# A hybrid mLSTM / DeltaNet decoder block: output travels on another DMA queue, and new due times for the steps of the triangular inverse

## The chip, the cores and the metric

The kernel runs on one core of a Trainium2 chip. TensorE (PE) multiplies matrices and loads its stationary operand (PEld); VectorE (DVE), ScalarE (ACT) and GpSimd (POOL) do the elementwise work; SyncE (SP) issues DMAs. [...] The metric is the device time of one execution in microseconds. The kernel before takes 2387.58 us (median of 3 runs, 2386.59 to 2389.55).

## The reference

One decoder layer over 512 tokens of width 2048, all in float32. The input is normalised and projected by one matrix `w_in`; the columns feed two token mixers and two merge gates.

```python
u = _rmsnorm(h, norm_w)
proj = jnp.matmul(u, w_in)
...
h_a = _mlstm_chunkwise(...)          # 8 heads, key width 128, value width 256
h_a = _merge_heads(_rmsnorm(h_a)) * ml_norm_w
h_a = h_a * jax.nn.sigmoid(ml_o) * jax.nn.silu(ml_z)

qkv = _causal_conv_silu(dn_qkv, dn_conv_w)   # width-4 causal convolution, then silu
dq, dk_ = _l2norm(dq), _l2norm(dk_)          # 16 heads of width 128
h_b = _gated_delta_chunkwise(dq, dk_, dv_, beta, g)
h_b = _merge_heads(_rmsnorm(h_b, dn_norm_w)) * jax.nn.silu(dn_z)

y_a = jnp.matmul(h_a, w_out[:ML_WIDTH])
y_b = jnp.matmul(h_b, w_out[ML_WIDTH:])
return sigmoid(gate_a) * y_a + sigmoid(gate_b) * y_b
```

The result is added to the input and normalised once more. The delta rule in a chunk needs the inverse of a unit lower triangular matrix, `I + A` with `A` made of the products of keys:

```python
a_mat = jnp.where(strict, bc[..., :, None] * kk * decay_mat, 0.0)
sol = lax.linalg.triangular_solve(a_mat + eye, rhs, lower=True, unit_diagonal=True)
```

## The kernel before

**Weights.** Every weight matrix is streamed once. A tile of 256 KB (`wr`) is loaded by SP, split into a high part `wh` by ACT (`split_hi`) and a rest `wl` by DVE (`split_lo`), and each product is made three times, high x high, high x low, low x high (L222 to L224, L252 to L254, L972 to L974). There are 768 such tiles, four buffers of `wr` and four of each part. The loop that emits the program loads four tiles and splits three tiles ahead of the one that PE is on.

**Units.** Work goes in units: four mLSTM units (two heads each) and eight DeltaNet units (two heads each), in the order m, d, d, m, d, d, and so on; so a DeltaNet unit is the first or the second of its pair. A unit projects its columns in blocks of eight weight tiles (`proj_cm`; in a DeltaNet unit K, Q, V, Z), where the two PSUM tiles of a block are taken from three buffers: the second head's first product of a block needs the first head's PSUM tile of the block before, which ACT must have copied out (`yp`, L451; `gz` and `thz`, L469 and L471). After the units come the merge gates (four narrow blocks, `proj_tm`, then six wide ones) and the output projection.

**Ticks.** The rest of a unit (norms, decay matrices, the inverse, the recurrences, output norm) is written as generators. `start(gen, wait)` files one, `tick()` is called after each half of a weight tile (six wide matmuls), and a generator's `yield n` asks to be resumed n ticks later. So the source says at which tick each small step is emitted. PE runs in exactly the order in which its instructions are emitted. For the other engines and for the DMA queues a planner reorders by its own estimates and by priority: `urgent()` raises it, `behind("A")` and `behind("V")` say that an instruction may not stand ahead of the newest split on ACT or DVE. Each queue then runs strictly in the planned order.

**A DeltaNet unit.** With tick 0 at the end of block K:
- `conv_silu` and `silu_end` (filed 3 and 5 ticks after their block for the two heads) make k, then `turn` makes a token-major copy. A turn is a transpose of 32 x 32 blocks on DVE, and then a trip through DRAM (`travel`): four stores `td` and, four ticks later, one load back. All of these DMAs are in SP's queue.
- `dn_front_k` makes the decay matrices, the products k·k (`pk`), the diagonal blocks `ls` (through DRAM, `ld`), and from tick 16 on the inverse of 128 small triangles, 31 steps of two DVE instructions each (`tmp`, `xi`; L573, L575). The result goes through DRAM (`xd`, L583; `tt`, L584), and 10 ticks later DVE turns it into `tn` (L587).
- `dn_front_q`, filed 8 ticks after block Q, makes the products k·q (`pqk`, L595).
- `dn_back`, filed 4 ticks after block Z, first takes the norms of q on ACT (`token_norms`, 64 squares in all units), then completes the inverse by four rounds of small products on PE (`p1` to `p4`; the first, L629, reads `tn`), with copies by ACT and DVE between them (`s1`, `tb`, `ta`, `s3`).
- `dn_chain` runs the recurrence of a head over its four chunks, normalises, and turns the output `os_` (`to`); `gated` multiplies it by the gate TURN ticks later and SP stores it to `h_d`.

**An mLSTM unit** ends in `ml_fin`, which turns two output tiles of each head (`mhn`) and files `gated` for each.

In all, 32 output tiles (16 `mhn`, 16 `to`) and 56 others (keys, queries, values) travel.

Of the kernel before, what the change touches and what calls it, by code (L numbers as in the profile page):

```python
# [17 lines left out]
NC = S // P  # L18
# [8 lines left out]
GNARROW = 4  # L27
GLAG = 3
KLAST = 4
TURN = 12  # L30
KWAIT, QWAIT = 4, 8
EPS = 1e-6
CAP = 15.0
MLH, DNH = 8, 16
# [5 lines left out]
BS = 32  # L40
# [8 lines left out]
def hybrid_body(  # L49
# [16 lines left out]
    nc = tc.nc  # L66
    ctx.enter_context(tc.manual_schedule(engines={mybir.EngineType.PE}))
    V, A, G, T = nc.vector, nc.scalar, nc.gpsimd, nc.tensor
# [51 lines left out]
    def behind(eng):  # L120

        return tc.issue_after(newest[eng])
# [56 lines left out]
    def urgent(level=1):  # L179
        return tc.high_priority(offset=level * PRIO)  # L180
# [4 lines left out]
    def start(gen, wait=0):  # L185
        active.append([gen, clock["t"] + wait])
# [242 lines left out]
    for i in range(NYP):  # L429
        t = wk.tile([P, S + 3], F32, tag=f"yp{i}", name=f"yp{i}", bufs=1)  # L430
# [13 lines left out]
    def bc(col, n):  # L444
        return col.unsqueeze(2).to_broadcast([P, NC, n])
# [11 lines left out]
    def silu_end(dst, then=None):  # L457
        th = wk.tile([P, S], F32, tag="th", name="th", bufs=3)
        with behind("A"):
            A.activation(th, dst, AF.Tanh)  # L460
        V.scalar_tensor_tensor(out=dst, in0=th, scalar=1.0, in1=dst, op0=ALU.add, op1=ALU.mult)
        if then is not None:
            turn(*then)
        yield 1
# [13 lines left out]
            with urgent():  # L478
                A.activation(jk, pk[:, c, :], AF.Square, accum_out=dst[:, c:c + 1])

    def turn(src, dst):


        o = dst if dst is not src else wk.tile([P, NC, P], F32, tag="to", name="to", bufs=2)
        V.transpose(o if len(src.shape) == 3 else o.rearrange("p n c -> p (n c)"), src)
        start(travel(o, dst), 2)

    def travel(o, dst):
        d = dr.tile([16, BS, 4, BS], F32, tag="td", name="td", bufs=8)
        ov = o.rearrange("p n (j c) -> p (n j) c", c=BS)  # L490
        with urgent(2):
            for a in range(4):
                nc.sync.dma_start(d[:, :, a, :].rearrange("m r c -> r m c"), ov[a * BS:(a + 1) * BS])
        yield 4
        with urgent(2):
            nc.sync.dma_start(dst, d.rearrange("(n j) r a c -> (j r) n (a c)", n=NC))
        yield 1

    def gated(hn, w, g, kt):
# [6 lines left out]
    def dn_front_k(hs, kq, u):  # L506
        rbs = [row_bcast(16 + h, "gb") for h in hs]
        yield 4
        for j in range(2):
# [1 line left out]
            G.affine_select(out=dm, in_=rbs[j], pattern=[[0, NC], [1, P]], channel_multiplier=-1, base=0,  # L511
                            compare_op=ALU.is_ge, fill=-1e30)
            u["dm"].append(dm)
        yield 2
        for j in range(2):
            h, rb, dm = hs[j], rbs[j], u["dm"][j]
            ge = wk.tile([P, NC], F32, tag="ge", name="ge", bufs=4)
# [50 lines left out]
        for i in range(BS - 1):  # L568
            n, m = BS - 1 - i, i // 4 + 1
# [11 lines left out]
        with urgent():  # L581
            for q in range(4):
                nc.sync.dma_start(xd[:, :, :, q, :].rearrange("g b m t -> (g b) m t"), xi[q * NSYS:(q + 1) * NSYS])  # L583
            nc.sync.dma_start(tt, xd.rearrange("g b m q t -> (b m q) g t"))  # L584
        yield 10
        with urgent(), behind("V"):
            V.transpose(tn.rearrange("p g m -> p (g m)"), tt.rearrange("p g t -> p (g t)"))  # L587
        u.update(tn=tn, tt=tt)
# [1 line left out]
    def dn_front_q(hs, kq, u):  # L590
        for j in range(2):
# [8 lines left out]
            G.tensor_tensor(out=qt, in0=qt, in1=eg, op=ALU.mult)  # L600
            u["qt"].append(qt)
            yield 1

    def dn_back(hs, kq, u):

        qe = wk.tile([P, 2, NC], F32, tag="qe", name="qe")
        with behind("A"):
            for j in range(2):
                token_norms(u["qn"][j], qe[:, j, :])
        V.tensor_scalar(out=qe, in0=qe, scalar1=EPS, scalar2=EPS * P, op0=ALU.add, op1=ALU.mult)  # L610
        u["qe"] = qe
        for j in range(2):
            ke = u["ke"][j]
            G.tensor_tensor(out=ke, in0=ke, in1=bc(u["dm"][j][0][:, :, P - 1], P), op=ALU.mult)


        tn, tt = u["tn"], u["tt"]
        G2 = [(j * NC + c, u["aq"][j][:, c, 0, :]) for j in range(2) for c in range(NC)]
        for b in range(4):
            bs = slice(b * BS, (b + 1) * BS)  # L620
            G.tensor_copy(tb[bs, :, bs], tt[bs])
        for b in range(2):
            bs = slice(b * BS, (b + 1) * BS)
            G.tensor_copy(ta[bs, :, bs], tn[bs])
        p1 = psw.tile([P, 2 * NC, BS], F32, tag="wk", name="p1")
        for g, a in G2:
            for q in range(2):
                a0, a1 = slice(64 * q, 64 * q + 32), slice(64 * q + 32, 64 * q + 64)
                T.matmul(p1[a1, g, :], a[a0, a1], tn[a0, g, :], start=True, stop=True)  # L629
        s1 = wk.tile([P, 2 * NC, BS], F32, tag="s3", name="s1", bufs=1)  # L630
        for q in range(2):
            a1 = slice(64 * q + 32, 64 * q + 64)
            with urgent():
                A.mul(s1[a1], p1[a1], -1.0)
        yield 2
        p2 = psw.tile([P, 2, 2 * NC, BS], F32, tag="wk", name="p2")
        for g, a in G2:
            for q in range(2):
                a0, a1 = slice(64 * q, 64 * q + 32), slice(64 * q + 32, 64 * q + 64)
                T.matmul(p2[a0, 0, g, :], s1[a1, g, :], tt[a1, g, :], start=True, stop=True)  # L640
            T.matmul(p2[32:64, 1, g, :], tt[32:64, g, :], s1[32:64, g, :], start=True, stop=True)
        for q in range(2):
            a0, a1 = slice(64 * q, 64 * q + 32), slice(64 * q + 32, 64 * q + 64)
            with urgent():
                A.copy(tb[a0, :, a1], p2[a0, 0])
        with urgent():
            V.tensor_copy(ta[32:64, :, 0:32], p2[32:64, 1])
        yield 2
        p3 = psw.tile([P, 2 * NC, 64], F32, tag="wk", name="p3")
        for g, a in G2:  # L650
            T.matmul(p3[64:128, g, :], a[0:64, 64:128], ta[:, g, :], start=True, stop=True)
        s3 = wk.tile([P, 2 * NC, 64], F32, tag="s3", name="s3", bufs=1)
        with urgent():
            A.mul(s3[64:128], p3[64:128], -1.0)
        yield 2
        p4 = psw.tile([P, 2 * NC, 64], F32, tag="wk", name="p4")
        for g, a in G2:
            T.matmul(p4[0:64, g, :], s3[64:128, g, :], tb[64:128, g, 64:128], start=True, stop=True)
        with urgent():
            V.tensor_copy(tb[0:64, :, 64:128], p4[0:64])  # L660
        for j in range(2):
            vn = u["vs"][j]
            with behind("V"):
                V.tensor_tensor(out=vn, in0=vn, in1=bc(u["nk"][:, j, :], P), op=ALU.mult)
        start(dn_chain(0, hs, kq, u), 2)
        start(dn_chain(1, hs, kq, u), 3)

    def dn_chain(j, hs, kq, u):
        h = hs[j]
        aq, qt, ke, ge = u["aq"][j], u["qt"][j], u["ke"][j], u["dm"][j][2]  # L670
# [5 lines left out]
        for c in range(NC):  # L676
            tsl = slice(c * P, (c + 1) * P)
            if st is None:
                r = vn[:, c, :]
            else:  # L680
                pr = psw.tile([P, P], F32, tag="wk", name="pr")
                T.matmul(pr, kq[j][:, 0, tsl], st, start=True, stop=True)
                r = wk.tile([P, P], F32, tag="r", name="r")
# [34 lines left out]
        os_ = wk.tile([P, NC, P], F32, tag="os", name="os")  # L718
        with urgent():
            V.tensor_tensor(out=os_, in0=po, in1=bc(rsd, P), op=ALU.mult)  # L720
        turn(os_, os_)
        start(gated(os_, normc[:, 32:33], u["g"][j], KT + h), TURN)

    def dn_unit(p):
        hs = (2 * p, 2 * p + 1)
        dcol = p * NB
        u = {"aq": [], "qt": [], "ke": [], "vs": [], "g": [], "dm": []}
        kq = [wk.tile([P, 2, S], F32, tag="kq", name=f"kq{h}", bufs=4) for h in hs]
        ps = proj_cm(DN_K + dcol)
        for j in range(2):  # L730
            ke = wk.tile([P, NC, P], F32, tag="ke", name="ke", bufs=4)
            u["ke"].append(ke)
            conv_silu(ps[j], 16 + hs[j], kq[j][:, 0, :])
            start(silu_end(kq[j][:, 0, :], (kq[j][:, 0, :], ke)), 3 + 2 * j)
        start(dn_front_k(hs, kq, u), 1)
        ps = proj_cm(DN_Q + dcol)
        u["qn"] = []
        for j in range(2):
            conv_silu(ps[j], hs[j], kq[j][:, 1, :])
            qn = wp.tile([P, NC, P], F32, tag="tg", name="qn", bufs=3)  # L740
            u["qn"].append(qn)
            start(silu_end(kq[j][:, 1, :], (kq[j][:, 1, :], qn)), 3 + 2 * j)
        start(dn_front_q(hs, kq, u), QWAIT)
        ps = proj_cm(DN_V + dcol)
        for j in range(2):
            vt = wk.tile([P, NC, P], F32, tag="vn", name="vt", bufs=4)
            u["vs"].append(vt)
            conv_silu(ps[j], 32 + hs[j], vt.rearrange("p c t -> p (c t)"))
            start(silu_end(vt.rearrange("p c t -> p (c t)"), (vt, vt)), 3 + 2 * j)
        ps = proj_cm(DN_Z + dcol)  # L750
        for j in range(2):
            g = wk.tile([P, S], F32, tag="g", name="gz", bufs=4)
            silu2(ps[j], g)
            u["g"].append(g)
        start(dn_back(hs, kq, u), 4)

    def ml_prep(j, hs, kq, u):
        h = hs[j]
# [72 lines left out]
    def ml_fin(j, hs, u):  # L831
        h = hs[j]
        hm = u["hm"][j]
        for i in range(2):
            hn = wk.tile([P, NC, P], F32, tag="os", name="mhn")
            turn(hm[i], hn)
            kt = 2 * h + i
            start(gated(hn, normc[:, 16 + kt:17 + kt], u["g"][j][i], kt), TURN)
            yield 1
# [118 lines left out]
    for nb in range(D // NO):  # L958
        nsl = slice(nb * NO, (nb + 1) * NO)
        for br in range(2):  # L960
# [3 lines left out]
            for c in range(NC):  # L964
                pool, t = (wp, "tg") if br == 0 or c == 3 else (bp, "tgb")
# [73 lines left out]
```

## Time and profile before

| what | us |
|---|---|
| median of 3 runs (lowest, highest) | 2387.58 (2386.59, 2389.55) |
| the profiled execution, its span | 2387.62, 2385.8 |
| PE busy | 2308.0 (97%) |
| DVE, ACT, POOL busy | 1146.0, 802.2, 198.2 |
| DMA: share of the 16 engines, over the span | 47.2%, 130 GB/s |
| mean granted TensorE clock | 0.988 |

The page gives the busy time of each engine; an engine is busy while one of its instructions runs, also when its clock is reduced. The list of waits says which instruction stood idle before it could start, what ended the wait, how long in total, how often, and the longest. A timeline line gives start, length, engine, source line, operation, output and inputs, and in brackets the idle time before it. SPq and ACTq are the DMA issues of those queues: their length is the time of the issue, not of the transfer.

The median time from issue to landing is 2.8 us for a weight tile, 2.7 us for one of the stores `td`, and 3.2 (`mhn`) or 3.6 us (`os`) for the load back of an output.

### The profile page before, as it was taken

Reading aid. Unit: us, or ns where it says so; the run is one execution under the profiler, and the core shown is the slowest. Engines: PE = TensorE matmul, PEld = TensorE weight load, DVE = VectorE, ACT = ScalarE, POOL = GpSimd, SP = SyncE. Lnnn points to the kernel's source line nnn. Section 1 sums busy time; section 2 is a strip of 40 time slices with the busy share of each in tenths; the row PEclk is TensorE's granted clock in tenths of the full one; section 3 lists DMA queues with packets and bytes.
Section 4 is the critical chain, followed back from the end, with each engine's and each line's share of the span. In section 5 each row is a group of like instructions: output and inputs, shape, how many; then the busy total and the mean of one; then the engine's idle time right before and its main releaser. Section 6 shows DMA issues by size and latency. Waiting matters only on the chain. (4 is left out here: it accounts for less than half of the span.)

```text
span 2385.8 us, 32124 instructions
## 1 busy us (share of the span) xinstructions
PE 2308.0 (97%) x11647; PEld 1926.1 (81%) x11647; DVE 1146.0 (48%) x2331; ACT 802.2 (34%) x1702; POOL 198.2 (8%) x277
## 2 busy tenths in 40 slices
PE   6999989999998999999899999989999999999998
PEld 5888877878887777888787888878998888888886
DVE  4532857533385743248583325857333222444334
ACT  4333333333333333233333324434333323322222
POOL 0000202100020200002020001111000000010010
PEclk9999999999999999999999999999999999999999
DMA  4433555443365645336563534646374533633333
GB/s 146 130 97 98 142 139 142 126 128 98 101 153 126 154 112 133 97 98 163 127 167 93 137 97 113 168 105 164 96 246 145 159 115 120 212 115 121 126 115 129
DMA packets 465441, 313.12 MB, mean 131 GB/s; under 512 B 234113, under 2 KB 404322, under 8 KB 465282
## 3 DMA queue, kind: packets, MB, share of 16 engines
q1 hardware_dynamic: 465218, 311.01, 47.2%
q8 instruction: 91, 1.49, 0.2%
q14 instruction: 68, 0.56, 0.1%
q10 hardware_dynamic: 64, 0.07, 0.0%
HBM read 264.77 MB, written 46.20 MB: 130 GB/s over the span
## 5 line engine op out<-in xcount | busy, mean ns | idle before, releaser
L118 DVE TENSOR_TENSOR wl<-wr,wh 128x512 fp32r<-128x512 f32 x768 | 547.3, 714 | 910.9 <-ACT wh L115 887.9
L115 ACT CAST wh<-wr 128x512 fp32r<-128x512 f32 x768 | 476.9, 622 | 1286.7 <-PE pj L223 586.4
L222 PE MATMUL pj<-uh,wh 128*128 128x512 f32 x1792 | 735.9, 411 | 13.3 <-ACT yp L451 7.9
L223 PE MATMUL pj<-ul,wh 128*128 128x512 f32 x1792 | 705.1, 393 | 0.3 <-DVE ul L304 0.3
L224 PE MATMUL pj<-uh,wl 128*128 128x512 f32 x1792 | 705.2, 394 | 0.0
L222 PEld LDWEIGHTS pj<-uh,wh 128*128 128x128 f32 x1792 | 340.5, 190 | 83.2 <-ACT yp L451 10.0
L224 PEld LDWEIGHTS pj<-uh,wl 128*128 128x128 f32 x1792 | 340.0, 190 | 74.1
L223 PEld LDWEIGHTS pj<-ul,wh 128*128 128x128 f32 x1792 | 341.1, 190 | 64.6 <-DVE ul L304 0.8
L972 PE MATMUL py<-wh,hh 128*128 128x512 f32 x512 | 199.2, 389 | 0.0
L973 PE MATMUL py<-wl,hh 128*128 128x512 f32 x512 | 199.2, 389 | 0.0
L974 PE MATMUL py<-wh,hl 128*128 128x512 f32 x512 | 199.2, 389 | 0.0
L253 PE MATMUL pg<-wl,uh 128*128 128x512 f32 x384 | 149.5, 389 | 0.2 <-DVE wl L118 0.2
L252 PE MATMUL pg<-wh,uh 128*128 128x512 f32 x384 | 149.5, 389 | 0.0
L254 PE MATMUL pg<-wh,ul 128*128 128x512 f32 x384 | 149.4, 389 | 0.0
L973 PEld LDWEIGHTS py<-wl,hh 128*128 128x128 f32 x512 | 96.1, 188 | 20.1
L974 PEld LDWEIGHTS py<-wh,hl 128*128 128x128 f32 x512 | 96.1, 188 | 19.9
L972 PEld LDWEIGHTS py<-wh,hh 128*128 128x128 f32 x512 | 96.1, 188 | 19.8
L252 PE MATMUL pv<-wh,uh 128*128 128x512 f32 x256 | 99.6, 389 | 0.0
L253 PE MATMUL pv<-wl,uh 128*128 128x512 f32 x256 | 99.6, 389 | 0.0
L254 PE MATMUL pv<-wh,ul 128*128 128x512 f32 x256 | 99.6, 389 | 0.0
L253 PEld LDWEIGHTS pg<-wl,uh 128*128 128x128 f32 x384 | 72.1, 188 | 15.3 <-DVE wl L118 0.5
L252 PEld LDWEIGHTS pg<-wh,uh 128*128 128x128 f32 x384 | 72.1, 188 | 15.1
(243 smaller groups left out, 2319.2 us busy)
## 6 DMA issues: line engine op xcount, KB each, us to landing
wr<-in_w_in_dram SPq DMA_DIRECT2D x640, 256.0 KB, 2.8
wr<-in_w_out_dram SPq DMA_DIRECT2D x128, 256.0 KB, 2.9
td<-to SPq DMA_DIRECT2D x128, 64.0 KB, 2.7
hr<-h_d SPq DMA_DIRECT2D x32, 256.0 KB, 3.4
tgl<-tg_d SPq DMA_DIRECT2D x32, 256.0 KB, 3.1
tg_d<-tgw SPq DMA_DIRECT2D x24, 256.0 KB, 3.3
xt<-in_x_dram SPq DMA_DIRECT2D x8, 512.0 KB, 8.2
gb<-rows_d SPq DMA_DIRECT2D x16, 256.0 KB, 3.5
```

What stands on the lines that cost most here:

```text
L115: newest["A"] = A.copy(hi, src).ins
L118: newest["V"] = V.tensor_tensor(out=lo, in0=src, in1=hi.bitcast(F32), op=ALU.subtract).ins
L222: T.matmul(ps[j], hi[:, k, wsl], uh[:, kt, :], start=(kt == 0), stop=False)
L223: T.matmul(ps[j], hi[:, k, wsl], ul[:, kt, :], start=False, stop=False)
L224: T.matmul(ps[j], lo[:, k, wsl], uh[:, kt, :], start=False, stop=(kt == KT - 1))
L252: T.matmul(ps[c], uh[:, kt, tsl], hi[:, 0, :], start=(kt == 0), stop=False)
L253: T.matmul(ps[c], uh[:, kt, tsl], lo[:, 0, :], start=False, stop=False)
L254: T.matmul(ps[c], ul[:, kt, tsl], hi[:, 0, :], start=False, stop=(kt == KT - 1))
L972: T.matmul(ps[c], hh[base][:, kt, tsl], hi[:, 0, :], start=(kt == 0), stop=False)
L973: T.matmul(ps[c], hh[base][:, kt, tsl], lo[:, 0, :], start=False, stop=False)
L974: T.matmul(ps[c], hl[base][:, kt, tsl], hi[:, 0, :], start=False, stop=(kt == KT - 1))
```

## The change

- `turn` takes a flag `out`. For the 32 output tiles the five DMAs of a travel are issued by ACT, each set tied behind ACT's newest split, and the travel begins 3 ticks after the transpose and no longer 2. The 56 other travels stay with SP.
- `dn_front_k` waits one tick more before its exponentials (2 to 3) and four more between the inverse's DMAs and `tn` (10 to 14).
- `dn_back` is filed 9 ticks after block Z, not 4.
- The norms of q move from `dn_back` to `dn_front_q`, 9 ticks after its second product; `dn_front_q` is filed at 9, not 8.
- The two `silu_end` of a block are filed at 4 and 7 ticks, not 3 and 5. TURN is 13, not 12.

No instruction is added or removed; 160 DMAs change their queue.

```diff
--- before.py
+++ after.py
@@ -27,8 +27,8 @@
 GNARROW = 4
 GLAG = 3
 KLAST = 4
-TURN = 12
-KWAIT, QWAIT = 4, 8
+TURN = 13
+QWAIT = 9
 EPS = 1e-6
 CAP = 15.0
 MLH, DNH = 8, 16
@@ -478,22 +478,24 @@
             with urgent():
                 A.activation(jk, pk[:, c, :], AF.Square, accum_out=dst[:, c:c + 1])
 
-    def turn(src, dst):
+    def turn(src, dst, out=False):
 
 
         o = dst if dst is not src else wk.tile([P, NC, P], F32, tag="to", name="to", bufs=2)
         V.transpose(o if len(src.shape) == 3 else o.rearrange("p n c -> p (n c)"), src)
-        start(travel(o, dst), 2)
-
-    def travel(o, dst):
+        start(travel(o, dst, out), 3 if out else 2)
+
+    def travel(o, dst, out):
+
         d = dr.tile([16, BS, 4, BS], F32, tag="td", name="td", bufs=8)
         ov = o.rearrange("p n (j c) -> p (n j) c", c=BS)
-        with urgent(2):
+        q = nc.scalar if out else nc.sync
+        with behind("A") if out else urgent(2):
             for a in range(4):
-                nc.sync.dma_start(d[:, :, a, :].rearrange("m r c -> r m c"), ov[a * BS:(a + 1) * BS])
+                q.dma_start(d[:, :, a, :].rearrange("m r c -> r m c"), ov[a * BS:(a + 1) * BS])
         yield 4
-        with urgent(2):
-            nc.sync.dma_start(dst, d.rearrange("(n j) r a c -> (j r) n (a c)", n=NC))
+        with behind("A") if out else urgent(2):
+            q.dma_start(dst, d.rearrange("(n j) r a c -> (j r) n (a c)", n=NC))
         yield 1
 
     def gated(hn, w, g, kt):
@@ -511,7 +513,7 @@
             G.affine_select(out=dm, in_=rbs[j], pattern=[[0, NC], [1, P]], channel_multiplier=-1, base=0,
                             compare_op=ALU.is_ge, fill=-1e30)
             u["dm"].append(dm)
-        yield 2
+        yield 3
         for j in range(2):
             h, rb, dm = hs[j], rbs[j], u["dm"][j]
             ge = wk.tile([P, NC], F32, tag="ge", name="ge", bufs=4)
@@ -582,7 +584,7 @@
             for q in range(4):
                 nc.sync.dma_start(xd[:, :, :, q, :].rearrange("g b m t -> (g b) m t"), xi[q * NSYS:(q + 1) * NSYS])
             nc.sync.dma_start(tt, xd.rearrange("g b m q t -> (b m q) g t"))
-        yield 10
+        yield 14
         with urgent(), behind("V"):
             V.transpose(tn.rearrange("p g m -> p (g m)"), tt.rearrange("p g t -> p (g t)"))
         u.update(tn=tn, tt=tt)
@@ -600,15 +602,16 @@
             G.tensor_tensor(out=qt, in0=qt, in1=eg, op=ALU.mult)
             u["qt"].append(qt)
             yield 1
-
-    def dn_back(hs, kq, u):
-
+        yield 9
         qe = wk.tile([P, 2, NC], F32, tag="qe", name="qe")
         with behind("A"):
             for j in range(2):
                 token_norms(u["qn"][j], qe[:, j, :])
         V.tensor_scalar(out=qe, in0=qe, scalar1=EPS, scalar2=EPS * P, op0=ALU.add, op1=ALU.mult)
         u["qe"] = qe
+
+    def dn_back(hs, kq, u):
+
         for j in range(2):
             ke = u["ke"][j]
             G.tensor_tensor(out=ke, in0=ke, in1=bc(u["dm"][j][0][:, :, P - 1], P), op=ALU.mult)
@@ -718,7 +721,7 @@
         os_ = wk.tile([P, NC, P], F32, tag="os", name="os")
         with urgent():
             V.tensor_tensor(out=os_, in0=po, in1=bc(rsd, P), op=ALU.mult)
-        turn(os_, os_)
+        turn(os_, os_, True)
         start(gated(os_, normc[:, 32:33], u["g"][j], KT + h), TURN)
 
     def dn_unit(p):
@@ -731,7 +734,7 @@
             ke = wk.tile([P, NC, P], F32, tag="ke", name="ke", bufs=4)
             u["ke"].append(ke)
             conv_silu(ps[j], 16 + hs[j], kq[j][:, 0, :])
-            start(silu_end(kq[j][:, 0, :], (kq[j][:, 0, :], ke)), 3 + 2 * j)
+            start(silu_end(kq[j][:, 0, :], (kq[j][:, 0, :], ke)), 4 + 3 * j)
         start(dn_front_k(hs, kq, u), 1)
         ps = proj_cm(DN_Q + dcol)
         u["qn"] = []
@@ -739,20 +742,20 @@
             conv_silu(ps[j], hs[j], kq[j][:, 1, :])
             qn = wp.tile([P, NC, P], F32, tag="tg", name="qn", bufs=3)
             u["qn"].append(qn)
-            start(silu_end(kq[j][:, 1, :], (kq[j][:, 1, :], qn)), 3 + 2 * j)
+            start(silu_end(kq[j][:, 1, :], (kq[j][:, 1, :], qn)), 4 + 3 * j)
         start(dn_front_q(hs, kq, u), QWAIT)
         ps = proj_cm(DN_V + dcol)
         for j in range(2):
             vt = wk.tile([P, NC, P], F32, tag="vn", name="vt", bufs=4)
             u["vs"].append(vt)
             conv_silu(ps[j], 32 + hs[j], vt.rearrange("p c t -> p (c t)"))
-            start(silu_end(vt.rearrange("p c t -> p (c t)"), (vt, vt)), 3 + 2 * j)
+            start(silu_end(vt.rearrange("p c t -> p (c t)"), (vt, vt)), 4 + 3 * j)
         ps = proj_cm(DN_Z + dcol)
         for j in range(2):
             g = wk.tile([P, S], F32, tag="g", name="gz", bufs=4)
             silu2(ps[j], g)
             u["g"].append(g)
-        start(dn_back(hs, kq, u), 4)
+        start(dn_back(hs, kq, u), 9)
 
     def ml_prep(j, hs, kq, u):
         h = hs[j]
@@ -833,7 +836,7 @@
         hm = u["hm"][j]
         for i in range(2):
             hn = wk.tile([P, NC, P], F32, tag="os", name="mhn")
-            turn(hm[i], hn)
+            turn(hm[i], hn, True)
             kt = 2 * h + i
             start(gated(hn, normc[:, 16 + kt:17 + kt], u["g"][j][i], kt), TURN)
             yield 1
```

## The prediction

> **What bounds the kernel now.** I read the page first, then PE's waits, then the clock in short windows, then the timelines of SP, DVE and ACT around the longest waits.
>
> ```profile
> PE 2308.0 (97%) x11647; PEld 1926.1 (81%) x11647; DVE 1146.0 (48%) x2331; ACT 802.2 (34%) x1702; POOL 198.2 (8%) x277
> ```
>
> TensorE is the bound: 97% busy, nothing else above half. Time is won only where PE waits or runs slowly. PE's waits (total, times, longest):
>
> ```profile
> PE p L629 <- DVE tn L587: 33.5, 8, 7.8
> PE pprm L103 <- DMA nrow<-in_ml_norm_w_dram: 15.2, 1, 15.2
> PE pj L222 <- ACT yp L451: 7.9, 5, 2.8
> PE pj L222 <- ACT thz L471: 4.8, 3, 2.1
> PE pqk L595 <- DVE kq L461: 0.6, 1, 0.6
> ```
>
> Of 66 us idle between matmuls, 15.2 is the start-up. 33.5 is one place, once per DeltaNet unit: the inverse's first product (L629) waits for `tn`. 12.7 (7.9 + 4.8) is at the first product of a projection block. The next view (window, length, busy time of PE, PEld, DVE, ACT, POOL, granted clock, DMA share, GB/s) shows what such a wait leaves behind:
>
> ```profile
> 519.50:522.90 3.40, 3.40 (x9) 2.68 (x9) 1.35 (x2) 0.62 (x1) 0.00 (x0) 0.50 0.82 245
> 741.40:748.20 6.80, 6.76 (x64) 5.08 (x66) 0.02 (x1) 1.37 (x3) 1.98 (x5) 0.50 0.01 4
> 600.00:610.00 10.00, 10.00 (x45) 8.26 (x45) 2.77 (x4) 2.50 (x4) 0.00 (x0) 1.00 0.32 102
> ```
>
> PE is busy in all three, but in the first two, right behind a wait, the clock is 0.50: 9 wide matmuls in 3.4 us against 45 in 10. A wait is therefore paid twice.
>
> Why `tn` is late, in the first unit. SP's queue, then DVE:
>
> ```profile
> 318.62 1.66 SPq L493 DMA_DIRECT2D td<-mhn  x3
> 320.39 0.43 SPq L152 DMA_DIRECT2D wr<-in_w_in_dram  x1
> 320.86 1.13 SPq L493 DMA_DIRECT2D td<-mhn  x2
> 322.08 0.50 SPq L496 DMA_DIRECT2D mhn<-td  x1
> 322.63 0.68 SPq L583 DMA_DIRECT2D xd<-xi  x1
> ...
> 324.81 2.13 SPq L583 DMA_DIRECT2D xd<-xi  x3
> ...
> 328.85 0.36 SPq L584 DMA_DIRECT2D tt<-xd  x1
> ```
>
> ```profile
> 317.98 0.17 DVE L575 TENSOR_TENSOR xi<-xi,tmp 128x8 f32<-128x8 f32 x1
> ...
> 331.30 0.45 DVE L587 STREAM_TRANSPOSE tn<-tt 128x256 f32<-128x256 f32 x1 [5.61 <-DMA tt<-xd]
> ```
>
> The inverse ends at 318.15, but its store `xd` waits 4.5 us on SP behind output travels (`td<-mhn`, `mhn<-td`), the read-back `mhn<-td` splits it, and `tn` ends at 331.75. PE stood from 324.0.
>
> The block-start waits have the same root. SP and ACT before PE's wait at 411.5:
>
> ```profile
> 402.41 2.21 SPq L493 DMA_DIRECT2D td<-qn  x4
> 404.67 0.51 SPq L496 DMA_DIRECT2D os<-td  x1
> 405.27 0.47 SPq L493 DMA_DIRECT2D td<-qn  x1
> 405.85 0.44 SPq L496 DMA_DIRECT2D os<-td  x1
> 406.33 1.75 SPq L493 DMA_DIRECT2D td<-qn  x3
> 408.18 0.56 SPq L496 DMA_DIRECT2D qn<-td  x1
> 408.78 1.61 SPq L152 DMA_DIRECT2D wr<-in_w_in_dram  x2
> ```
>
> ```profile
> 412.98 0.62 ACT L115 CAST wh<-wr 128x512 fp32r<-128x512 f32 x1 [7.80 <-DMA wr<-in_w_in_dram]
> 413.50 0.58 ACT L451 COPY yp<-pj 128x512 f32<-128x512 f32 x1
> ```
>
> No weight load left SP from 400.1 to 408.8 while these eleven travel DMAs and more did; ACT stood 7.8 us in front of a split, and the PSUM copy `yp` that PE needed was queued behind it.
>
> **The change, part by part.** The sum is made against the profiled execution, 2387.6 us (span 2385.8 and 1.8 around it); the median of the three runs is the same 2387.6. A tick is six wide matmuls; 24 of them start in 5.44 us (317.99 to 323.43), so 1.36 us a tick.
>
> *Inverse.* `tn` is issued five ticks later (yield 2 to 3, 10 to 14) and its consumer `dn_back` too (4 to 9), so the gain is not between those two: it is that both move 5 x 1.36 = 6.8 us behind the arithmetic, which moves one tick at most. Replay of the first unit: in the built order `xd` no longer has travels ahead, but one weight load sits before its last quarter, so stores from 319.0 to 322.0; the wait for landing as before (324.81+2.13 to 328.85, 1.9) gives `tt` at 323.9; `tn` ends 2.9 after that's issue, at 326.8. PE now asks at 324.0 + 6.8 = 330.8. Margin 4 us, 2.6 if the arithmetic is a tick later. The four second units waited 5.0 in all (33.5 less the first units' 7.8, 7.0, 6.6, 7.2), 0.4 to 2.2 each, under 6.8. Gain: 33.5.
>
> *Clock behind them.* Half clock while PE worked: 3.4 (331.8 on), 6.8 (741.4), 3.4 (854.0), 5.9 (1151.9), 6.3 (1557.7): 25.8 us, half of it lost: 12.9.
>
> *Output travel to ACT.* 32 tiles x (4 `td` + 1 read-back) = 160 DMAs leave SP's queue. The row of `td` on SP has a median of 0.49 us, so SP is freed of 78 us. Weight loads, `xd`, and the other travels move up. Gain: the block-start waits 12.7 and their half clock, (3.0 + 3.4)/2 = 3.2; 15.9.
> ACT gains those 160 issues. Its own queue shows three DMAs, 0.27 to 0.51 us: 43 to 82 us, up to 0.82 each (131) by SP's slowest bunch (5 `td` in 4.11); I take 0.49, 78, as the SP row is the same transfer. ACT would be at 880 of 2330, 38%. The cover is its lead: ACT waited 586 us for PE to return buffers in L223's blocks alone. What is queued behind a travel: the next split (three tiles, 8.2 us, ahead), DVE's `wl` behind that, and a block's PSUM copies. Each travel waits for its transpose on DVE, and a read-back for its four stores (2.7 us to landing). The tight place is the V block of a second unit: the transposes end near 404, two travels and the read-backs end near 409, `yp` is due by 411.4. Bounds 0 to 2.8 us (the longest such wait now) at four places; I take 2 in all, as 0 fits the replay.
>
> *DVE stands for `tt`.* In the new order `tn` sits behind the Z block's second gate and 100 splits, reached near 321, so DVE idles until 326.4 (before, too: 29.1 us in all). Behind it stands the `wl` of tile 100, then done at 327.5 to 328.9; PE needs it at 330.8 - 1.36 = 329.4. Bounds 0 to 2 at four places; taken 2 in all.
>
> *Later silu ends* (3, 5 to 4, 7 ticks). The second head's k·k product keeps 2 ticks of cover instead of 3, k·q 3 instead of 4 (QWAIT 8 to 9): 1.36 us less where the wait was 0.6 once. 0 to 1.4 at eight places; taken 2 in all. In exchange ACT's `th` stands less in front of unfinished convolutions.
>
> *q norms.* 64 squares with their accumulator reads, 8 per unit, 3.5 us (321.66 to 325.3, less a split), leave the place before `s1` for the start of the Z block; they need `qn`, landed seven ticks before. No PE work waits for them in either place: nothing, covered by ACT's lead; bare it would be 3.5 x 8 = 28.
>
> *Tail.* The last outputs end about six ticks later, so the narrow gate blocks give way to the loads of `h` and x one block (16 ticks) later; the x loads bunch as now, where ACT waited 3.2 us for `wr` and PE 0.2. Bounds 0 to 3; taken 1. Half clock behind all these leftovers: 1.
>
> Sum: 33.5 + 12.9 + 15.9 = 62.3, less 2 + 2 + 2 + 1 + 1 = 8: 54.3 us. 2387.6 - 54.3 = 2333.3.
>
> The trace puts half clock behind waits of 1.9 (850.8), 2.1 (516) and 2.6 us (411.5), but not behind 2.8 (821.8) or 1.9 (928). [...]
>
> **The rivals.**
> 1. *The inverse stays late* (0.14). Its store still shares the 16 DMA engines with the travels (share 0.92 to 1.0 from 320 to 326). If `tn` comes 4 us later than replayed, the first units wait 2.5 us and 1.7 of half clock: 4 x 4.2 = 17, 2350.
> 2. *The loads stay late* (0.12). DMA share is 0.98 to 1.13 between 408 and 412: if engines, not SP's issue, starve the weights, the 15.9 stays and the 2 is part of it: 2347. Against: from 400.1 to 408.8 no load was issued at all. [...]
> 3. *ACT becomes the wait* (0.07; slower). In each of 16 pairs of travels ACT stands for the transposes (SP's longest wait for one: 3.6) and issues at 0.82: 2 x (3.6 + 3.3) = 13.8 us against a lead of 8.2; PE loses 5.6 and 1.7 of clock, 16 x 7.3 = 117: 2450. It decides from 54.3/16 = 3.4 us a pair. Against: `mhn` is transposed well before its travel, and ACT's lead is seldom used.
> 4. *It doesn't do what it says* (0.04): SP's other travels (`vt`, `qn`) still hold `xd`; 33.5 and 12.9 stay: 2387.6 - 15.9 + 8 = 2380; in half of this case the block waits stay too, 2388.
> 5. *No leftovers* (0.05): 2325.
>
> **How the numbers follow.** Forecast 0.58, 2325 to 2341 by the leftovers' bounds. With 1, 2 and 5 the range is 2322 to 2354. Faster by over 0.2% (4.8 us, about what a measurement tells): 0.91; slower 0.07 (rival 3); same 0.02, half of rival 4.
>
> **What would show it.** PE's wait at the inverse's first product under 4 us in all; no granted clock of 0.50 after the start outside single windows of 3.4 us; `xd` issued within 1.5 us of the inverse's end; ACT's wait for `wr` well under 100.8; about 160 DMAs on ACT's queue near 0.5 us each. Wrong: ACT waiting for `to` or `td` with PE behind it, or new `wl` waits near the fourth tile after Z.

## The result and the profile after

The changed kernel takes 2320.70 us (2319.34 to 2321.74); the kernel before, run beside it, 2387.09 (2385.83 to 2389.55). The ratio is 0.972, with a 95% interval of 0.9704 to 0.9737: faster by 66 us. The forecast was 2333, 2322 to 2354; the time lies 1.3 us below its low end. The profiled execution took 2320.75 us (span 2318.9), against 2387.62 before: 66.9 us less, and those have to be found.

Busy time, from the page of the kernel after:

```profile
PE 2288.7 (99%) x11647; PEld 1916.7 (83%) x11647; DVE 1143.9 (49%) x2331; ACT 803.6 (35%) x1702; POOL 191.9 (8%) x277
```

PE is busy for 19 us less with the same 11647 matmuls, so part of the gain is matmuls that run faster. PE's waits (total, times, longest):

```profile
PE pprm L103 <- DMA nrow<-in_ml_norm_w_dram: 15.4, 1, 15.4
PE put L302 <- DVE xt L294: 2.4, 1, 2.4
PE pj L222 <- ACT uh L303: 0.6, 1, 0.6
PE pj L223 <- DVE ul L304: 0.3, 1, 0.3
PE pgt L345 <- ACT gr L329: 0.3, 1, 0.3
```

All five belong to the start-up. The waits for `tn`, `yp` and `thz` are gone. The clock from the start-up to the tail (window, length, busy time of PE, PEld, DVE, ACT, POOL, granted clock, DMA share, GB/s):

```profile
28.30:2311.00 2282.70, 2279.09 (x11618) 1909.40 (x11616) 1126.62 (x2294) 785.93 (x1677) 188.03 (x262) 1.00 0.48 133
```

There is no half clock any more between 28 us and the tail. The path of the first unit's inverse, in the timelines of SP, DVE and PE:

```profile
315.67 1.96 SPq L585 DMA_DIRECT2D xd<-xi  x3
317.67 0.60 SPq L152 DMA_DIRECT2D wr<-in_w_in_dram  x1
318.32 0.56 SPq L585 DMA_DIRECT2D xd<-xi  x1
320.91 0.37 SPq L586 DMA_DIRECT2D tt<-xd  x1
```

```profile
323.76 0.45 DVE L589 STREAM_TRANSPOSE tn<-tt 128x256 f32<-128x256 f32 x1 [3.91 <-DMA tt<-xd]
```

```profile
329.55 0.39 PE L224 MATMUL pj<-uh,wl 128*128 128x512 f32 x1
329.87 0.69 PE L632 MATMUL p<-tn,aq 32*32 32x32 f32 x32
```

The inverse ends at 314.53 and its store leaves 1.1 us later, with one weight load ahead of the last quarter, as replayed. `tn` ends at 324.2 and PE comes for it at 329.9: 5.7 us to spare, where it stood 7.8 us before (4.0 to 6.5 us in the four first units, 6.6 to 7.4 in the second ones). And the second unit's V block, SP and then ACT, where before eleven travels and more held the loads from 400.1 to 408.8:

```profile
381.77 1.98 SPq L495 DMA_DIRECT2D td<-qn  x4
383.85 0.46 SPq L152 DMA_DIRECT2D wr<-in_w_in_dram  x1
...
385.76 2.91 SPq L152 DMA_DIRECT2D wr<-in_w_in_dram  x2
...
390.44 3.55 SPq L495 DMA_DIRECT2D td<-qn  x4
394.19 0.39 SPq L152 DMA_DIRECT2D wr<-in_w_in_dram  x1
```

```profile
387.60 1.99 ACTq L495 DMA_DIRECT2D td<-to  x4
389.83 0.62 ACT L115 CAST wh<-wr 128x512 fp32r<-128x512 f32 x1 [3.02 <-PE pj L223]
391.35 2.15 ACTq L495 DMA_DIRECT2D td<-to  x4
...
397.00 0.62 ACT L115 CAST wh<-wr 128x512 fp32r<-128x512 f32 x1 [2.78 <-DMA wr<-in_w_in_dram]
397.77 0.59 ACT L451 COPY yp<-pj 128x512 f32<-128x512 f32 x1
```

The longest stretch without a load in it is 5.5 us (388.7 to 394.2), and ACT's splits wait 11.9 us for `wr` in all, where it was 100.8.

**Where the 66.9 us went.** PE's idle time between matmuls falls from 66.2 us to 19.0: 47.2. The half clock behind waits, 32.2 us of work in the profile of before, cost half of that, 16.1. The tail is 0.3 shorter. Most of the other 3.3 belongs to the waits themselves: a wide matmul has a modelled length of 0.39 us but the next starts after 0.227, so a wait, which is counted from the modelled end, costs its idle time and 0.16 more. Nineteen waits went: 3.0; the rest, 0.3, is not placed.

### The profile page after: what moved, and what is told of

It reads as the page before. It is cut to its first block, busy times and chain, and to the rows that moved or that the text cites. A ratio compares the mean times of both kernels' runs of the same rounds, so it can differ in the third digit from the quotient of the medians.

```text
span 2318.9 us, 32199 instructions
## 1 busy us (share of the span) xinstructions
PE 2288.7 (99%) x11647; PEld 1916.7 (83%) x11647; DVE 1143.9 (49%) x2331; ACT 803.6 (35%) x1702; POOL 191.9 (8%) x277
## 4 chain that ended last, share of the span: by engine, by line
PE 98%; DMA 1%; DVE 0%; SPq 0%; issue 0%; ACT 0%; POOL 0%; DVEq 0%; POOLq 0%; ACTq 0%
PE pj L222 18%; PE pj L223 18%; PE pj L224 18%; PE py L975 5%; PE py L976 5%; PE py L977 5%; PE pg L254 4%; PE pg L253 4%; PE pg L252 4%; PE pv L252 3%; PE pv L253 3%; PE pv L254 2%; PE pjt L237 1%; PE pjt L240 1%; PE pjt L239 1%; PE pk L535 1%
## 5 line engine op out<-in xcount | busy, mean ns | idle before, releaser
L252 PEld LDWEIGHTS pg<-wh,uh 128*128 128x128 f32 x384 | 72.1, 188 | 14.9
```

The costliest lines, as they stand in the source:

```text
L252: T.matmul(ps[c], uh[:, kt, tsl], hi[:, 0, :], start=(kt == 0), stop=False)
```

## The experiments

All were timed beside the kernel before, which took 2384.1 to 2386.0 us (medians) in those comparisons. Waits are PE's, from each kernel's profile; "block" is `yp` and `thz` together. A profile shows one execution; in e_queue, e_spread, e_back1 and e_qn12 it was the shortest of those timed, so the usual waits there may be longer.

| kernel | median us | ratio (95%) | `tn` us | block us |
|---|---|---|---|---|
| after | 2320.70 | 0.9720 (0.9704 to 0.9737) | 0 | 0 |
| e_queue | 2346.50 | 0.9835 (0.9820 to 0.9850) | 12.9 | 3.0 |
| e_ticks | 2322.53 | 0.9737 (0.9721 to 0.9753) | 1.6 | 0 |
| e_norms | 2320.05 | 0.9728 (0.9713 to 0.9742) | 0 | 0 |
| e_silu | 2324.08 | 0.9744 (0.9729 to 0.9759) | 0 | 2.7 |
| e_slack | 2319.82 | 0.9727 (0.9711 to 0.9743) | 1.8 | 0 |
| e_spread | 2381.86 | 0.9987 (0.9978 to 0.9996) | 35.2 | 8.8 |
| e_back1 | 2382.31 | 0.9992 (0.9983 to 1.0001) | 42.8 | 0.4 |
| e_short | 2339.95 | 0.9815 (0.9801 to 0.9830) | 0.5 | 10.9 |
| e_shift | 2385.24 | 0.9997 (0.9985 to 1.0010) | 32.2 | 13.0 |
| e_late | 2321.05 | 0.9733 (0.9719 to 0.9748) | 0.6 | 0 |
| e_chain | 2325.09 | 0.9753 (0.9739 to 0.9768) | 1.1 | 0 |
| e_yield | 2378.91 | 0.9976 (0.9965 to 0.9986) | 33.3 | 8.8 |
| e_qn12 | 2380.82 | 0.9981 (0.9968 to 0.9993) | 35.1 | 3.7 |

**The queue alone (e_queue)**: the kernel before, with the output travels on ACT.

```diff
-        start(travel(o, dst), 2)
+        start(travel(o, dst, out), 2)
...
+        q = nc.scalar if out else nc.sync
+        with behind("A") if out else urgent(2):
```

> The kernel before with one part of the change: the 32 output travels are issued by ACT, tied behind its splits; every tick stays as before. Theory (the queue is the main part): the block-start waits go (12.7 us and 3.2 of half clock), and the store of the inverse is no longer held, so that tn ends some 86.5 us after the unit's first PSUM copy, as in the changed kernel, while PE asks at 85.4 (92.2 less five ticks): 1 to 3 us of wait in the four first units, under 1 in the second ones, 8 in all, with little half clock. Time 2330 to 2340. Rival (the slack is what counts): PE's wait for tn stays above 20 us in all, time 2355 to 2372.

```profile
PE p L630 <- DVE tn L588: 12.9, 8, 2.8
PE pj L222 <- ACT yp L451: 3.0, 5, 1.6
PE p L652 <- DVE ta L648: 2.2, 2, 1.4
```

39 us of the 66; the time lies between the ranges of the two theories. Both kinds of wait shrink, neither goes: `tn` is still late in all eight units, by 2.8 us at most. The waits for `thz` are gone, and of the 7.5 us for `yp` in the second units' V blocks 0.65 is left; the other 2.4 us for `yp` stand in first units, where it was 0.45 before. A small new wait appears, for `ta`. The profile has no half clock ahead of the tail; its execution took 2342.3 us at a mean granted clock of 0.999, the other three 2345.5 us and more at 0.995 to 0.996.

**The change without the queue (e_ticks)**: the output travels go back to SP.

```diff
-        q = nc.scalar if out else nc.sync
-        with behind("A") if out else urgent(2):
+        q = nc.sync
+        with urgent(2):
```

> The changed kernel with the output travels back in SP's queue; every new tick stays. Theory: PE asks for tn 6.8 us later, which covers all but 0 to 1 us of each first unit's wait and all of the second units'; the block-start waits of about 12.7 us and their half clock stay, as SP still bunches its travels in front of the weight loads. PE waits for tn 0 to 4, at block starts 10 to 16 in all; time 2338 to 2346. Rival (each part alone removes everything): PE waits under 5 us in all, 2321 to 2325. Rival (the slack does little while the store is held): PE waits for tn above 15, time above 2355.

1.8 us above the change, with intervals that overlap: the time of the rival, that each part alone removes everything, and not of the theory. No block-start wait comes back although all 88 travels share SP's queue again. What the queue buys is the margin: in three first units `tn` ends 0.1 to 0.9 us ahead of PE's request and in the other it comes 1.6 us late, where with ACT's queue it is 4.0 to 6.5 us ahead. So the ascription of the block-start waits to the queue is in doubt, and the next runs go after that.

**The norms back in dn_back (e_norms)**

```diff
-        yield 9
+
+    def dn_back(hs, kq, u):
+
```

> The changed kernel with the q norms back in front of the inverse's last steps. Theory: nothing waits for them, ACT's lead covers their 3.5 us a unit: 2318 to 2323, PE's waits as in the changed kernel. Rival: they stand in front of the first scaled copy of the inverse on ACT, PE waits 1 to 3.5 us for it in each of eight units: 2329 to 2350.

No wait comes back and the time is the same. The move is worth nothing, as costed.

**The silu ends back (e_silu)**: 3 + 2j ticks and QWAIT 8 in the changed kernel.

```diff
-            start(silu_end(kq[j][:, 0, :], (kq[j][:, 0, :], ke)), 4 + 3 * j)
+            start(silu_end(kq[j][:, 0, :], (kq[j][:, 0, :], ke)), 3 + 2 * j)
```

> The changed kernel with the silu ends at 3 and 5 ticks and the k.q products at 8, as before. Theory: no PE wait in either form, 2318 to 2323. Rival: the later silu ends are what keeps ACT's queue free (its tanh stood 70 us in front of unfinished convolutions before), so that block-start waits of 3 to 10 us come back: 2325 to 2335.

Five waits for `yp`, 2.7 us in all, and 3.4 us of time; the intervals just overlap. ACT's splits, behind a read-back that waits for its four stores of `to`, stand 54.5 us in all, where it is 22.9 in the change. So with the travels on ACT the later silu ends seem to do some work; the theory, no wait in either form, missed.

**The slack alone (e_slack)**: the kernel before with five ticks more for the inverse; queue, norms, silu ends and TURN as before.

```diff
-        yield 2
+        yield 3
...
-        yield 10
+        yield 14
...
-        start(dn_back(hs, kq, u), 4)
+        start(dn_back(hs, kq, u), 9)
```

> The kernel before with the inverse's ticks alone (2 to 3, 10 to 14, and its last steps 4 to 9): queue, silu ends, norms and TURN as before. Theory now (the later last steps do nearly all; the block-start waits come from travels that meet in one queue, and it is enough to move them apart in time): the outputs travel later and the queries not, so that they part only halfway: PE waits for tn 0 to 4, at block starts 2 to 8, time 2324 to 2338. Rival (five ticks alone do it): 2321 to 2324, no block-start wait. Rival (block-start waits need the silu ends or the queue): 10 to 13 us of them stay with their half clock, 2336 to 2342.

2319.82: the whole gain, with every travel in SP's queue; the rival, that five ticks alone do it, came nearest, its range 1.2 us too high. The rest of the change adds nothing that can be measured to it.

**The spread alone (e_spread)**: the later silu ends, QWAIT 9 and the first yield of 3.

```diff
-            start(silu_end(kq[j][:, 0, :], (kq[j][:, 0, :], ke)), 3 + 2 * j)
+            start(silu_end(kq[j][:, 0, :], (kq[j][:, 0, :], ke)), 4 + 3 * j)
```

> The kernel before with the silu ends at 4 and 7 ticks, the k.q products at 9 and the one tick before the decay exponentials: no slack for the inverse, no new queue. Theory: PE's wait for tn stays near 33 us with its half clock (12.9); block-start waits fall somewhat, to 4 to 12; 2372 to 2388. Rival (less bunching also lets the inverse end sooner): the wait for tn under 20, 2345 to 2365.

3 to 4 us, and the waits for `tn` stay: these ticks alone are not enough.

**The request moved forward (e_back1)**: the changed kernel, with dn_back filed at 1 instead of 9.

```diff
-        start(dn_back(hs, kq, u), 9)
+        start(dn_back(hs, kq, u), 1)
```

> The changed kernel with the last steps filed 1 tick after block Z and not 9: PE asks for tn eight ticks, 10.9 us, sooner; everything else as changed. It measures what a wait costs. In the changed kernel PE asked 5.7 us after tn was there (first units) and 7 us after (second units), so waits of about 5 and 4 us are due, 36 in all. [...] Rival (a wait costs its own length): 2357 to 2360, no granted clock of 0.50.

```profile
PE p L632 <- DVE tn L589: 42.8, 8, 7.1
```

All the gain is gone. The eight waits are 4.3 to 7.1 us long, and each is followed by half clock (seven stretches of 6.8 us and one of 10.2, part of each still inside the wait; the mean granted clock is 0.986, where it is 0.998 in the change). The span is 59.4 us longer for 42.8 us of waiting: these waits cost 1.4 times their length. At its own length alone, 42.8 us, the time would have been 2363.5.

**A shorter inverse (e_short)**: are the block-start waits an echo of PE's 7 us stall at the inverse? The kernel before leaves out the inverse's last 8 steps, so that `tn` is in time; the inverse's own DMAs leave sooner, and every other tick stays.

```diff
-        for i in range(BS - 1):
+        for i in range(BS - 9):
...
-        yield 10
+        yield 14
```

> The kernel before, with the last 8 of the inverse's 31 steps left out (so its output is not the reference's) and tn issued at the same tick as before: the inverse's result is ready about 5 us sooner, and nothing else of the ticks, the queues or the chain moves. Theory A (place): the block-start waits come from where the output travels stand in SP's queue, whatever the inverse does. Then PE's wait for tn goes to under 2 us, yp and thz stay near 12.7 us in 8 waits, and the time is 2387 - 33.5 - 12.9 - 1.3 (eight restarts of 0.16) = 2339 us. Theory B (echo): the block-start waits are an after-effect of the 7 us stall at the inverse, which leaves the other engines out of step with the written order. Then they go as well and the time is near that of the slack alone, 2320 to 2324.

```profile
PE pj L222 <- ACT yp L451: 7.2, 4, 2.5
PE pj L222 <- ACT thz L471: 3.7, 3, 1.7
...
PE p L629 <- DVE tn L587: 0.5, 2, 0.3
```

2339.95 against 2339 worked out by theory A. The echo falls: without the stall the block-start waits are still 10.9 us of 12.7. It also prices the late `tn` by itself: 45 us with its half clock and restarts. Of the remaining 19 us down to the change, the block-start waits account for 15.4 (10.9, 3.4 of half clock and seven restarts of 0.16); the rest was not taken apart.

**The output DMAs later (e_shift)**: the kernel before, with the travels of `to` filed 7 ticks after the transpose and TURN 17.

```diff
-        turn(os_, os_)
+        turn(os_, os_, 7)
```

> The kernel before, with the travel of the 16 DeltaNet outputs (td from to, and the load back) filed 7 ticks after the transpose instead of 2, the gate 5 ticks later too; inverse, dn_back and SP's queue as before. Theory A (place): PE's block-start waits shrink from 12.7 to under 3 us, because the four td no longer meet the travels of qn while to is still late on DVE; the waits for tn stay near 33.5 with their half clock; 2387 - 10 to 13 - 2 to 3 - 1 = 2371 to 2374. Theory B (echo): tn's stall is untouched, so the block-start waits stay: 2385 to 2389.

```profile
PE pj L222 <- ACT yp L451: 13.0, 4, 4.0
```

Theory A missed here: the three waits for `thz` went, but those for `yp` grew from 7.9 to 13.0. From 397.9 to 409.2 us SP issued 19 travel DMAs of the outputs and of q with no weight load between: the two still met, later and in a longer bunch. Place matters, but moving the DMAs of the outputs is not enough.

**The stores of the inverse held back (e_late)**: e_slack with five of the ticks ahead of `xd`.

```diff
+        yield 5
         with urgent():
             for q in range(4):
                 nc.sync.dma_start(xd[...
...
-        yield 14
+        yield 9
```

> The slack alone (dn_back 5 ticks later, yields 3 and 14 in all), but the stores xd of the inverse held back for 5 of the ticks: the late inverse is put back, while chain and output travels stay at their new place. In the first units tn was ready within 0.5 us of PE's request, so it is now 6 to 7 us late there; in the second units the 7 us to spare are used up. PE waits 24 to 30 us for tn. Theory A (place): no block-start waits (under 1.5 us in all); time 2320 + 1.4 x 27 = 2358 (2353 to 2364). Theory B (echo): the block-start waits return with it, 10 to 13 us and their half clock: 2370 to 2378.

Neither number came, because the edit did not do what it was meant to: in the first unit `xd` left SP at 319.3 and 321.7 us, in e_slack at 319.4 and 321.6. It was already behind the travels of `mhn` and a weight load. This run decides nothing between the theories.

**The chain's place alone (e_chain)** and **the inverse's yields alone (e_yield)**: e_slack taken apart.

```diff
-        start(dn_back(hs, kq, u), 4)
+        start(dn_back(hs, kq, u), 9)
```

> The kernel before with dn_back, and so the recurrence and its output travels, filed 9 ticks after block Z instead of 4; the inverse's own two yields stay at 2 and 10. Theory A2 (the chain's place): both kinds of wait hang on where dn_back and the chain stand against the projection blocks. PE asks for tn 6.8 us later, so the first units wait 0 to 1 us each; and the written order of SP's queue has the first head's q travel (td from qn) one weight load ahead of the output travels instead of in one bunch of 15 DMAs with them, so the block-start waits are under 1.5 us: 2320 to 2326. Rival C (the inverse's yields): the front of the inverse, one tick later, is what gives DVE room ahead of the wait for ls; without it yp and thz stay near 12.7 and the time is 2336 to 2342.

```diff
-        yield 2
+        yield 3
...
-        yield 10
+        yield 14
```

> The kernel before with the two yields of dn_front_k alone (2 to 3 ahead of the exponentials, 10 to 14 ahead of tn); dn_back stays at 4. Theory A2 (the chain's place): nothing is gained. PE still waits 30 to 36 us for tn and 10 to 14 us at block starts, and SP's written order still has the bunch of 15 travel DMAs after one weight load: 2383 to 2390. Rival C (the inverse's yields): the block-start waits go and those for tn stay: 2366 to 2373.

One number, 4 to 9, gives 60 of the 66 us and removes both kinds of wait but for 1.1 us on `tn`. The yields alone give 6 us, a little more than theory A2 allowed, and leave both. Rival C falls. In e_chain, SP's second V block fits theory A2: q's first travel goes out a weight load ahead of the rest, and SP stands less for a late `to` (4.8 us in all, where it was 17.5).

```profile
385.44 1.96 SPq L493 DMA_DIRECT2D td<-qn  x4
387.50 0.44 SPq L152 DMA_DIRECT2D wr<-in_w_in_dram  x1
388.93 0.38 SPq L496 DMA_DIRECT2D qn<-td  x1
389.40 0.46 SPq L152 DMA_DIRECT2D wr<-in_w_in_dram  x1
390.24 0.32 SPq L493 DMA_DIRECT2D td<-to  x1
...
398.20 0.50 SPq L152 DMA_DIRECT2D wr<-in_w_in_dram  x1
```

Still 8.3 us without a load, but two loads left just ahead of it. Before, one load left in the 14.9 us from 393.9 to 408.8.

**The travels of q out of the bunch (e_qn12)**: the kernel before, with the travels of q filed 12 ticks after their transpose.

```diff
-            start(silu_end(kq[j][:, 1, :], (kq[j][:, 1, :], qn)), 3 + 2 * j)
+            start(silu_end(kq[j][:, 1, :], (kq[j][:, 1, :], qn, 12)), 3 + 2 * j)
```

> The kernel before with the travels of q alone filed 12 ticks after their transpose instead of 2; outputs, chain and inverse as before. In SP's written order the bunch between two weight loads in the second unit's V block shrinks from 15 DMAs (td from to and qn, os and qn back) to 5, and SP still stands for the late transpose of the output ahead of it. Theory (a), the bunch: the weight loads leave in time, PE's block-start waits fall from 12.7 to under 4 us, the waits for tn stay at 30 to 36: 2370 to 2376. Theory (b), the stand for the output's transpose: yp and thz stay at 10 to 14 us and the time is 2382 to 2389.

```profile
PE p L629 <- DVE tn L587: 35.1, 8, 6.4
...
PE pj L222 <- ACT thz L471: 3.7, 3, 1.5
```

```profile
394.52 1.97 SPq L493 DMA_DIRECT2D td<-to  x4
396.59 0.45 SPq L152 DMA_DIRECT2D wr<-in_w_in_dram  x1
397.14 2.16 SPq L493 DMA_DIRECT2D td<-to  x4
399.40 0.44 SPq L496 DMA_DIRECT2D os<-td  x1
399.89 1.11 SPq L152 DMA_DIRECT2D wr<-in_w_in_dram  x2
```

The waits for `yp`, all but 0.45 us of which lay in second units' V blocks, are gone, with the outputs in SP's queue, at their old ticks, and with SP's stand for `to` as long as before (17.5 us, longest 3.6). So there the bunch of both kinds of travel is the cause, and not the stand. The waits for `thz`, in the mLSTM unit that follows (515 us and the like), stay at 3.7 of 4.8. There the outputs meet another kind, the travels of the mLSTM keys (`kw`). The kernel before:

```profile
503.04 2.15 SPq L493 DMA_DIRECT2D td<-kw  x4
505.24 2.71 SPq L493 DMA_DIRECT2D td<-to  x5
508.06 1.01 SPq L496 DMA_DIRECT2D kw<-td  x2
```

From 498.1 to 510.2 us SP issued 20 travels of the two without a weight load. In e_qn12, which leaves both at their ticks, the same 20 stand from 496.8 to 508.3; in e_shift the outputs come behind the keys and a weight load leaves after every four or five travels (494.9, 498.2, 502.4, 507.1), and no wait for `thz` is left.

Little of the time came. The profiled execution took 2374.0, as expected; the median of ten is 2380.8, above the range of theory (a) and below that of (b), and where the difference lies in the other nine is not seen. In the profile part of the gain moved on to the next wait: the second units' waits for `tn` grew from 5.0 to 11.7 us, while those of the first units fell from 28.6 to 23.4.

## Why the prediction was right or wrong

**Direction and mechanism of the main gain: right.** The replay of the inverse held in its order (one load ahead of the last quarter of `xd`; the store 1.1 us behind the inverse's end) and the wait of 33.5 us went. Its size was cautious: the inverse itself ended 3.6 us sooner than in the profile of before, so the margin in the replayed unit is 5.7 us and not 4 (in the other first units 4.0 to 6.5).

**Half clock: right.** 12.9 + 3.2 forecast, 16.1 found by the same count; e_back1 shows the price from the other side.

**"Output travel to ACT ... Gain: the block-start waits 12.7 and their half clock": the right bunch, the wrong share.** Taking the outputs out of SP's queue does remove nearly all of these waits where they stood (e_queue). But it is not needed: the tick of dn_back alone leaves none, with the travels on SP. The bunch was read as too many DMAs in one queue, while it was two kinds of travel that met there, and moving either kind can part them: e_qn12 does it for q and the outputs, e_shift for the keys and the outputs, though in the V blocks e_shift made it longer. And the sum gave 15.9 us to the queue and 46.4 (33.5 + 12.9) to the ticks, as if parts added up; alone they give 39 and 66. The total did not suffer because the change holds both, which is luck. The same step's rest held: ACT's queue costs 0.44 and 0.52 us a store (medians for `mhn` and `to`; 0.49 was taken), ACT stands 31.8 us for the stores (22.9 + 8.9), and PE waits for none of it.

**"Sum: 33.5 + 12.9 + 15.9 = 62.3, less ... 8": the step whose size failed.** Every leftover was nil: no new wait in the V block, none for `tt` or `wl`, none for the silu ends, none at the tail. They were chosen inside bounds whose low end was 0, although the replay gave 0 for the V block and showed `wl` done ahead of PE's need. That alone would have left the time at 2325.3, inside the range. The 62.3 itself lacked 4.5, and that took it past the low end: the restart of 0.16 for each of nineteen waits (3.0), the small waits for `pqk`, `pcs` and `pg` (1.2) and the tail (0.3). 54.3 + 8 + 4.5 = 66.8.

**The q norms: right**, nothing (e_norms). **The later silu ends** were charged 2; undoing them costs 3.4 us with the travels on ACT.

**The rivals.** 1 (the inverse stays late) fell: `tn` is 4.0 to 7.4 us ahead of PE in all eight units. 2 (the loads stay late) fell: the splits' wait for `wr` is 11.9. In e_queue, issuing the same 160 DMAs from a second queue, behind ACT's splits, was worth 39 us, and the weight loads had waited behind SP's issues of 0.49 us each (median of `td`). No run separates these issues from SP's stand for late outputs in that gain. 3 (ACT becomes the wait) fell at 32 tiles. 4 fell. 5 (no leftovers, 2325) was the nearest, at a chance of 0.05.

## What to carry to other kernels

When a queue runs in order, look at which transfers meet in it, and move the cheapest one to move: one due time on the consumer's side gave 60 of the 66 us here. Test an edit's parts alone before ascribing gains: the parts overlapped (the slack 66, the queue 39, the spread 3 to 4 us alone; 66 together). Where a replay of the new order shows no leftover, take none as the likeliest, and count a removed wait with its restart (0.16 us each here) and the half clock behind it (16.1 us in all here).

## What the runs showed of the hardware

**Half clock started on a grid.** In the profile of before, seven stretches of half clock stand ahead of the tail. They start at 328.37, 413.70, 519.51, 737.96, 854.02, 1147.56 and 1553.75 us: 25, 31, 64, 34, 86 and 119 steps of 3.413 us apart. They last one (three times), two (once) or three steps (three times), and the one of the tail, at 2376.36, starts on the same grid. The prediction was puzzled by a wait of 2.8 us without half clock and one of 1.9 us with it. The kernel before, cut on its grid:

```profile
410.29:413.70 3.41, 1.25 (x6) 0.71 (x4) 1.61 (x8) 0.72 (x2) 0.00 (x0) 1.00 0.83 248
413.70:417.11 3.41, 2.97 (x7) 2.39 (x8) 3.38 (x9) 1.83 (x4) 0.00 (x0) 0.50 0.97 317
...
819.86:823.27 3.41, 1.98 (x9) 1.31 (x7) 2.72 (x9) 0.00 (x0) 0.00 (x0) 1.00 1.02 270
823.27:826.69 3.42, 2.06 (x9) 1.72 (x10) 2.53 (x8) 2.11 (x4) 0.00 (x0) 1.00 0.93 246
826.69:830.10 3.41, 3.41 (x17) 2.83 (x16) 3.41 (x8) 1.65 (x3) 0.34 (x1) 1.00 1.10 377
```

The wait of 2.60 us at 411.5 puts 2.16 into one step, and the next step runs at 0.50. The longer wait of 2.80 at 821.8 straddles a boundary, 1.4 in each step, and nothing follows. In this profile, from 28 us to the tail, no step at full clock with 1.5 us of idle PE or less was followed by half clock (the most is 1.5, at 1256.8), and each of the seven with 1.85 or more was (the least is the wait of 1.85 at 850.8, all in one step). Two more steps: one with 1.58 in e_queue (719.75) was not, one with 2.53 in e_short (401.5) was. So here it was not the length of a wait alone that told whether half clock followed, but also where in the steps it fell.

**The kernels with such waits scattered more.** Those without waits of this size repeat within 3 us (after: 2319.3 to 2321.7; e_slack: 2319.3 to 2321.8), those with eight or more of them within 6 to 11 (e_qn12: 2374.0 to 2385.3; e_shift: 2378.8 to 2390.1; ten runs each against four). The cause is not shown: there is one trace of each kernel.
